# A transformer block on one core: out-projection by seven block products, and two norms left to the scales of later stages

## The chip, the cores and the metric

The kernel runs on one core of one Trainium2 chip. The metric is the device time of one execution in microseconds (us). TensorE multiplies (PE in the profile, with its weight loads as PEld), VectorE (DVE) and ScalarE (ACT) do elementwise work, GpSimd (POOL) does a little elementwise work and issues accumulating DMAs, and SyncE (SP) issues the other DMAs.

## The reference, cut to what matters

512 tokens of width 2048, 256 memory tokens, all float32. Three sub-layers, each with a norm before and a norm after it:

```python
h = rms_norm(x, g_mix_pre);  proj = h @ w_in            # 16 heads of 128
mix = concatenate([out_a, out_b], -1) @ w_out            # out-projection
x = x + rms_norm(mix, g_mix_post)
h = rms_norm(x, g_mem_pre)                               # cross-attention: 4 heads of 512
s_ = einsum(h @ w_mq, rms_norm(mem, g_mem_kv) @ w_mkv[keys]) * 512 ** -0.5
o = (softmax(s_) @ values) @ w_mo
x = x + rms_norm(o, g_mem_post)
h = rms_norm(x, g_ffn_pre)
gu = h @ w_gate_up
f = (silu(gu[:, :D_FF]) * gu[:, D_FF:]) @ w_down         # D_FF = 5632
x = x + rms_norm(f, g_ffn_post)
```

`rms_norm(x, g)` is x times 1/sqrt(mean(x*x) + eps) of its row, times g by column.

## The kernel before

Every fp32 operand is held as a high and a low part in fp32r, and a product is three matmuls in sequence: high by high, high by low, low by high. The making of such a pair is called a split: a copy on ScalarE and a subtraction on VectorE. Weights come in chunks of 128x1024 (512 KB). The class `Weights` loads them in a fixed order into five buffers (`NR`; eight from the end of cross-attention on) and splits each two chunks ahead of its use; `mm` (L218) issues the matmuls.

The stages are, in order: keys and values of the memory tokens, 16 attention heads, out-projection (about 880 to 1024 us in the profile), cross-attention (to about 1410) and the feed-forward part (FFN).

- **Out-projection.** `tok_ticks` runs over 4 blocks of 512 output columns by 8 weight chunks by 4 tiles of 128 tokens. The last column block is done twice over, for tiles 0 and 1 and then for tiles 2 and 3, and its eight chunks are loaded twice. `split_mix` splits the heads' outputs. `Sub.evict` squares the result for the norm behind it and multiplies by the gain `g_mix_post`.
- **The chain of a token tile** (`Sub.chain`): `residual` makes the row's 1/rms (`r1`, a power on POOL), adds x and squares the sum; `normed` makes the second 1/rms (`r2`) and, by column block, `h = y * r2 * gain` (L843, VectorE), the next sub-layer's normed input; `turn` transposes it on TensorE (L852) and splits it.
- **Cross-attention.** `fold_keys` multiplies `w_mq` by the keys (16 folds of 24 matmuls 128x256 for a pair of heads; in pair 0 the chains run between them), then come the scores, the softmax, `fold_values` (values by `w_mo`) and `cross_out`, which does all four tiles of a column block at once, and in the last column block one tile after the other, with a chain behind each.
- **FFN.** `Blocks` multiplies a 2x2 block matrix by seven products instead of eight (Strassen's method, Winograd's form): sums of blocks of the activations and of the weights first, sums of the products behind them. A block is 256 tokens by 1024 inputs by 512 columns; a product is 48 matmuls of 128x512. Weight sums are formed by accumulating DMAs, which POOL issues, or by VectorE.

Each engine works its instructions off in a fixed order. The order is set when the program is built: the code is written with generators (`side`, `side2`) that are advanced one step at each `fill()` between matmuls, and a scheduler merges what results.

Of the kernel before, what the change touches and what calls it, by code (L numbers as in the profile page):

```python
# [53 lines left out]
HOMES = {1: (0, 0), 2: (1, 0), 5: (0, 1), 6: (1, 1)}  # L54
# [4 lines left out]
SY, SZ = 5, 2  # L59
# [6 lines left out]
G_MIX, G_KV, G_DIFF, G_SB, G_ALL = 0, 16, 32, 33, 34  # L66

GP_MIX, GP_MEM, GP_FFN, GP_MEM_PRE, GP_FFN_PRE = range(5)


class Weights:
# [5 lines left out]
    def __init__(self, nc, raw, parts, chunks):  # L77
        self.nc, self.parts, self.chunks = nc, parts, chunks
        self.free = deque(raw[:, i] for i in range(NR))
# [10 lines left out]
    def more(self, tiles, mark):  # L90

        for t in tiles:
            self.nc.vector.tensor_copy(t[:, 0:1], mark[:, 0:1])
            self.free.append(t)

    def load(self, last):
        while self.loaded <= min(last, len(self.chunks) - 1):
            n = self.loaded
            _, how, *src = self.chunks[n]
            if how == "load":  # L100
                if not self.free:
                    return
                t = self.free.popleft()
                self.nc.sync.dma_start(t, src[0])
                for x in src[1:]:
                    self.nc.gpsimd.dma_start(t, x, accum_op=ALU.add)
                self.raw[n] = t
            self.loaded += 1

    def split(self, n):  # L110
        if n < len(self.chunks):
            r = self.raw.pop(n)
# [5 lines left out]
            if n in self.sums:  # L118
                m = self.sums[n]
                t = self.raw[m] = self.held.pop(self.chunks[m][2])  # L120
                self.nc.vector.tensor_tensor(t, t, r, op=ALU.add)
            if n in self.adds:
                m = self.adds[n]
                self.nc.gpsimd.dma_start(r, self.chunks[m][3], accum_op=ALU.add)  # L124
                self.raw[m] = r
            elif n in self.kept:
                self.held[n] = r
            else:
                self.free.append(r)
# [14 lines left out]
class Side:  # L144

    def __init__(self):
        self.q = deque()
        self.wait = 0  # L150
# [4 lines left out]
    def force(self):  # L155
        try:
            self.wait = next(self.q[0]) or 0
# [3 lines left out]
    def step(self):  # L161
        if self.wait:
            self.wait -= 1
        elif self.q:
# [5 lines left out]
    def drain(self):  # L170
        while self.q:
            self.force()
        self.wait = 0
# [3 lines left out]
def encoder_kernel(ctx: ExitStack, tc: tile.TileContext, a: dict, out: bass.AP):  # L177
# [69 lines left out]
    def wf(name, cbs, c0, n, order, make, again=False):  # L247
# [6 lines left out]
        for i in order:  # L254
            how, *x = make[i]
            for c in range(n):
                key = (name, cbs, c0 + c)
                if how == "load":
                    x_ = (block(c, *x[0]),)
# [15 lines left out]
    dn_cbs = [(0, 1), (2, 3)]  # L275
# [8 lines left out]
    for cb in range(NCB):  # L284
        wm("w_out", cb, range(8))
    wm("w_out", NCB - 1, range(8))
# [8 lines left out]
    for b, n in enumerate(DOWN):  # L295
        for cbs in dn_cbs:
            if (b, cbs) == (len(DOWN) - 1, dn_cbs[-1]):
# [11 lines left out]
    def fill():  # L309
        if later:  # L310
            later.popleft()()
        side.step()
        side2.step()
# [213 lines left out]
    mixT, mixhl = {}, {}  # L527
# [77 lines left out]
    def subnorm(o, head, g):  # L605
# [7 lines left out]
        yield 2  # L613
# [10 lines left out]
        m = u(s="mixT")  # L624
        nc.vector.scalar_tensor_tensor(m, ob, g, t, op0=ALU.mult, op1=ALU.mult)
        mixT[head] = m
        if head == 0:
            mixhl[0] = (u(F32R, "mixh"), u(F32R, "mixl"))
            split(*mixhl[0], mixT.pop(0))
# [72 lines left out]
    def sb_gen(h, q, k, v):  # L702
# [30 lines left out]
        yield SY  # L733
# [35 lines left out]
    def split_mix(kt):  # L769
        m = mixT.pop(kt)  # L770
        split(big[:, 0, kt], big[:, 1, kt], m)
        mixhl[kt] = from_big(kt)

# [3 lines left out]
    class Sub:  # L777
# [3 lines left out]
        def __init__(self, gp, src, dst, gpre, raw=None):  # L781
            self.gp, self.src, self.dst, self.gpre = gp, src, dst, gpre
            self.raw = raw
# [8 lines left out]
        def load_g(self, cb):  # L792
# [4 lines left out]
            if self.gpre is not None and cb == NCB - 1:  # L797
                self.gpre_rows = []
                for c in range(NCB):
                    t = u(s="gpre")  # L800
                    dma(t, a["grows"][self.gpre, c * 512 : (c + 1) * 512].partition_broadcast(P))
                    self.gpre_rows.append(t)
# [14 lines left out]
        def residual(self, t, steps=False):  # L817
# [5 lines left out]
            for cb in range(NCB):  # L823
                if cb == 2 and steps:
                    yield
                y, x = self.y[t, cb], self.x.pop((t, cb))
                if self.gpre is None and t >= NT - 2 and cb == 0:
# [4 lines left out]
                if self.gpre is not None:  # L832
# [3 lines left out]

        def normed(self, t, ss2):
            s2, r2 = st(), st()
            nc.vector.tensor_reduce(s2, ss2, axis=AX.X, op=ALU.add)
            pow_rstd(r2, s2, 1)  # L840
            for cb in range(NCB):
                h = u(s="h")
# [657 lines left out]
```

## Time and profile before

| What | Value |
|---|---|
| median of 3 runs | 2742.3 us (2740.06 to 2749.47) |
| the profiled execution | 2740.57 us, of which the span of the profile is 2738.8 |
| TensorE busy | 2674.0 us, 98% of the span |
| VectorE, ScalarE, GpSimd busy | 60%, 47%, 8% |
| mean granted TensorE clock | 0.991 of full speed |

The 1.8 us between the execution and the span lie around the profiled part. Waits of TensorE and stretches at a lower clock are what the span holds beside matmuls at full speed; the rows further down show them by stage.

### The profile page before, as it was taken

The numbers are of one execution on the slowest core, as the hardware profiler recorded it, in microseconds if no ns is written. First come the engines' busy times: TensorE is split into PE (matmuls) and PEld (weight loads), VectorE is DVE, ScalarE is ACT, GpSimd is POOL, SyncE is SP. The second block draws the span as 40 slices with busy tenths as digits, with TensorE's granted clock in tenths as the row PEclk, the third lists the DMA queues.
The fourth block names the chain that finished last, engine by engine and source line by source line (L and its number), as shares of the span: only waits on it lengthen the run. The fifth ranks groups of instructions, "written<-read, shape, count | busy, mean of one in ns | idle before, by whom it ended". The sixth has DMA issues, their size and how long they took to land.

```text
span 2738.8 us, 33641 instructions
## 1 busy us (share of the span) xinstructions
PE 2674.0 (98%) x12704; PEld 2220.3 (81%) x12704; DVE 1642.1 (60%) x2267; ACT 1296.7 (47%) x1908; POOL 230.7 (8%) x273
## 2 busy tenths in 40 slices
PE   8999999999999998999989999999999999999996
PEld 7888877888887788988877888888888888878775
DVE  6763555554444357335377655555555568787887
ACT  6542444445455345324365444444444456454553
POOL 0000000000000000000011122111121121101101
PEclk9999999999999999999999999999999999999998
DMA  8873222222222375223368999888888998778776
GB/s 304 293 255 98 84 89 85 81 82 76 81 73 74 115 249 193 67 100 124 113 202 188 252 207 209 205 205 204 206 195 208 200 229 247 208 251 206 197 206 204
DMA packets 163715, 470.14 MB, mean 172 GB/s; under 512 B 18272, under 2 KB 28920, under 8 KB 163552
## 3 DMA queue, kind: packets, MB, share of 16 engines
q1 hardware_dynamic: 128928, 346.45, 37.4%
q0 software_dynamic: 34624, 121.54, 24.1%
q8 instruction: 99, 1.62, 0.2%
q14 instruction: 64, 0.52, 0.1%
HBM read 431.20 MB, written 39.34 MB: 172 GB/s over the span
## 4 chain that ended last, share of the span: by engine, by line
PE 89%; issue 4%; DVE 3%; DMA 2%; ACT 1%; POOL 1%; SPq 0%; POOLq 0%; DVEq 0%; ACTq 0%
PE ps L218 88%; DVE parts L116 1%; PE ps L1251 1%; DMA aq<-actT_d 1%; PE ps L852 1%; ACT parts L115 1%; DMA xnat<-in_x_dram 1%; DMA raw<-in_w_dn_dram 0%; DVE y L831 0%; PE ps L689 0%; POOL y_d L1367 0%; DMA xres<-x_d 0%; DMA raws<-in_w_mk_dram 0%; DVE big L222 0%; DVE form L222 0%
## 5 line engine op out<-in xcount | busy, mean ns | idle before, releaser
L218 PE MATMUL ps<-parts,big 128*128 128x512 f32 x4992 | 1170.7, 392 | 12.9 <-ACT parts L115 7.0
L218 PEld LDWEIGHTS ps<-parts,big 128*128 128x128 f32 x4992 | 935.2, 188 | 214.6 <-DVE parts L116 9.5
L116 DVE TENSOR_TENSOR parts<-raws,parts 128x1024 fp32r<-128x1024 f32 x551 | 672.8, 1223 | 612.4 <-ACT parts L115 604.3
L115 ACT CAST parts<-raws 128x1024 fp32r<-128x1024 f32 x551 | 579.7, 1052 | 768.2 <-PE ps L218 698.8
L218 PE MATMUL ps<-parts,form 128*128 128x512 f32 x2376 | 551.3, 390 | 2.5 <-ACT parts L115 2.3
L218 PEld LDWEIGHTS ps<-parts,form 128*128 128x128 f32 x2376 | 444.5, 188 | 96.9 <-ACT parts L115 4.5
L218 PE MATMUL ps<-big,parts 128*128 128x512 f32 x1536 | 375.1, 394 | 0.0
L218 PEld LDWEIGHTS ps<-big,parts 128*128 128x128 f32 x1536 | 282.6, 188 | 61.9 <-issue 4.2
L116 DVE TENSOR_TENSOR parts<-raw,parts 128x1024 fp32r<-128x1024 f32 x175 | 213.8, 1223 | 150.7 <-ACT parts L115 150.5
L115 ACT CAST parts<-raw 128x1024 fp32r<-128x1024 f32 x175 | 184.3, 1054 | 203.5 <-PE ps L218 161.6
L218 PE MATMUL ps<-memhl,parts 128*128 128x512 f32 (+1 forms) x1024 | 182.1, 339 | 7.9 <-DVE memhl L229 7.3
L218 PEld LDWEIGHTS ps<-memhl,parts 128*128 128x128 f32 x1024 | 157.6, 190 | 31.7 <-DVE memhl L229 7.6
L124 POOL DMA_DIRECT2D raws<-in_w_gu_dram x112 | 96.8, 864 | 897.5 <-DVE parts L116 683.3
L369 POOL TENSOR_TENSOR small<-small 128x1 f32<-128x1 f32 (+2 forms) x22 | 16.8, 770 | 991.8 <-DVE small L368 976.4
L218 PE MATMUL ps<-khl,parts 128*128 128x256 f32 x768 | 96.9, 287 | 0.0
L218 PEld LDWEIGHTS ps<-khl,parts 128*128 128x128 f32 x768 | 94.6, 194 | 0.2
L218 PE MATMUL ps<-gh,big 128*128 128x512 f32 x256 | 80.0, 393 | 0.0
L218 PE MATMUL ps<-big,pTh 128*128 128x512 f32 x256 | 79.6, 390 | 0.0
L124 POOL DMA_DIRECT2D raw<-in_w_gu_dram x60 | 51.8, 864 | 111.5 <-DVE parts L116 111.5
L666 ACT ACTIVATE e<-e,small 128x512 f32<-128x512 f32 (+3 forms) x64 | 35.4, 555 | 54.2 <-DVE small L664 54.2
L814 DVE TENSOR_TENSOR y<-ps,gpost 128x512 f32<-128x512 f32 x32 | 22.0, 690 | 58.2 <-ACT junk L812 57.6
L218 PEld LDWEIGHTS ps<-gh,big 128*128 128x128 f32 x256 | 48.6, 190 | 10.1
(781 smaller groups left out, 2138.1 us busy)
## 6 DMA issues: line engine op xcount, KB each, us to landing
raws<-in_w_gu_dram POOLq DMA_DIRECT2D x113, 512.0 KB, 5.6
raws<-in_w_gu_dram SPq DMA_DIRECT2D x79, 512.0 KB, 4.3
raws<-in_w_qk_dram SPq DMA_DIRECT2D x64, 512.0 KB, 3.3
raw<-in_w_gu_dram POOLq DMA_DIRECT2D x63, 512.0 KB, 5.6
raw<-in_w_gu_dram SPq DMA_DIRECT2D x57, 512.0 KB, 4.1
aq<-actT_d SPq DMA_DIRECT2D x82, 256.0 KB, 5.8
raws<-in_w_dn_dram SPq DMA_DIRECT2D x41, 512.0 KB, 5.1
raws<-in_w_out_dram SPq DMA_DIRECT2D x40, 512.0 KB, 3.6
```

Source lines behind the costliest of these rows:

```text
L115: self.nc.scalar.copy(h, r)
L116: self.nc.vector.tensor_tensor(l, r, h.bitcast(F32), op=ALU.subtract)
L124: self.nc.gpsimd.dma_start(r, self.chunks[m][3], accum_op=ALU.add)
L218: nc.tensor.matmul(o, l, r, start=start, stop=stop, skip_group_check=True)
L369: nc.gpsimd.tensor_tensor(dst, t, mhalf[:, 0:n], op=ALU.pow)
L666: nc.scalar.activation(es[m][:, 0:n], es[m][:, 0:n], AF.Exp, bias=nmx[:, m : m + 1], accum_out=z[:, m : m + 1],)
L814: nc.vector.tensor_tensor(y, p, self.g[cb], op=ALU.mult)
L852: nc.tensor.transpose(tp[:, k * P : (k + 1) * P], h[:, k * P : (k + 1) * P], ident)
L1251: nc.tensor.transpose(tp[:, k * P : (k + 1) * P], f[:, k * P : (k + 1) * P], ident)
```

## The change

Three things change:

1. **The out-projection goes through `Blocks`.** Its columns are two pairs of blocks, `(0, 1)` and `(2, 3)`; each pair takes seven products of 48 matmuls. Products 1 and 7 of both pairs come first (`EARLY`), then 2, 3, 5, 6 and 4 of pair 0 and then of pair 1. The heads' outputs stay in 16 tiles `mix` of 128x2x256; `mix_forms` makes the activation blocks' sums, the subtractions on POOL (`sub_p`). Weights of products 7 and 5 are formed by a load and an accumulating DMA, of product 6 by VectorE, of product 4 by an accumulating DMA on what 6 used. Three more buffers (`mraw`) join once product 7 of pair 1 is out, until the out-projection ends. Behind the products, sums with product 7 (`last`) and the gain for tiles 2 and 3 run on POOL.
2. **No normed input is formed.** The rows `h` (L843) and the loads of their gains are gone. `turn` transposes the residual sum itself. The gain `g_mem_pre` is folded into the scale with which `fold_keys` splits its result, and `r2` becomes the scale of the softmax's exponent; `g_ffn_pre` is applied when the transposed tile leaves PSUM (a VectorE multiplication in the place of a ScalarE copy), and `r2` in the Silu's scale and in the gated product. A chain handles one tile and yields for stated times (`CH`) instead of numbers of steps.
3. **Cross output by tiles.** Column blocks 0 and 1 are done for all tiles as before, then blocks 2 and 3 for tile 0, then for tile 1, then block 2 and then block 3 for tiles 2 and 3. The subtractions of `late_forms` (FFN forms of tiles 2 and 3) move from VectorE to POOL.

```diff
-HOMES = {1: (0, 0), 2: (1, 0), 5: (0, 1), 6: (1, 1)}
+HOMES = {1: (0, 1), 2: (1, 1), 5: (0, 0), 6: (1, 0)}
+EARLY, ORDER_MIX = (1, 7), (2, 3, 5, 6, 4)
+MAKE_MIX = {1: ("load", (0, 0)), 7: ("load", (1, 1), (0, 1)), 2: ("load", (1, 0)),
+            3: ("load", (1, 1)), 5: ("load", (0, 0), (0, 1)), 6: ("sum", 3, 5),
+            4: ("add", 6, (1, 0))}
+CH = 8.0, 2.0
...
-        m = u(s="mixT")
-        nc.vector.scalar_tensor_tensor(m, ob, g, t, op0=ALU.mult, op1=ALU.mult)
+        for th in range(2):
+            if head % 2 == 0:
+                mix[head // 2, th] = u2(F32, "mix")
+            r = slice(th * M, (th + 1) * M)
+            nc.vector.scalar_tensor_tensor(
+                mix[head // 2, th][:, head % 2], ob[:, r], g, t[:, r],
+                op0=ALU.mult, op1=ALU.mult,
+            )
...
-        def normed(self, t, ss2):
...
-                nc.scalar.copy(self.raw[cb, t], tp)
+                nc.vector.tensor_tensor(
+                    h.rearrange("p (a b) -> p a b", a=4),
+                    tp.rearrange("p (a b) -> p a b", a=4),
+                    gain.unsqueeze(2).to_broadcast([P, 4, P]),
+                    op=ALU.mult,
+                )
...
+        def chain(self, t):
+            ss2 = yield from self.residual(t, True)
+            yield CH[0]
+            for cb in range(NCB):
+                self.turn(t, cb)
+                if cb == NCB - 1:
+                    s2, r2 = st(), st()
+                    nc.vector.tensor_reduce(s2, ss2, axis=AX.X, op=ALU.add)
+                    pow_rstd(r2, s2, 1)
+                    self.r2[t] = r2
+                yield CH[1]
...
+                    def last():
+                        nc.gpsimd.tensor_tensor(v, v, w, op=ALU.add)
+                        nc.gpsimd.tensor_tensor(r, r, w, op=ALU.add)
...
+    def mix_forms():
+        for k2 in range(1, 4):
+            mix_form(1, k2, mix[k2, 0])
+            yield 2
+        for k2 in range(4):
+            t = u2(F32, "s7")
+            sub_p(t, mix[k2, 1], mix[k2, 0])
+            mix_form(7, k2, t)
+            yield 2
+        for k2 in range(4):
...
+            a11, a12, a21, a22 = (mix.pop((k2 + 4 * c, r)) for r in range(2) for c in range(2))
+            mix_form(2, k2, a12)
+            sub_p(a21, a21, a22)
...
+            sub_p(a11, a11, a21)
...
+            sub_p(a12, a12, a11)
...
+            (nc.vector if t < 2 else nc.gpsimd).tensor_tensor(c, c, sub.g[cb], op=ALU.mult)
+            sub.y[t, cb] = c
+            if cb == col_pairs[-1][t < 2]:
+                (side, side2)[t // 2].add(sub.chain(t))
...
+    for i in EARLY:
+        for n, g in enumerate(pairs):
+            g.product(i)
+            done_mix.add((i, n))
+    mix_raw = [wpool.tile([P, 1024], F32, tag=f"mraw{i}", name=f"mraw{i}") for i in range(NR, NW)]
+    W.more(mix_raw, pairs[1].T[7, 1], n_mix)
...
-        split_scaled(gh, gl, p, 512 ** -0.5)
+        split_scaled(gh, gl, p, gmem[:, r : r + 1])
...
-            sub2(s, a21, a22)
+            sub_p(s, a21, a22)
...
+    for toks, cbs in (((0,), last), ((1,), last), ((2, 3), last[:1]), ((2, 3), last[1:])):
...
-            nc.scalar.activation(g, g, AF.Silu)
-            nc.vector.tensor_tensor(f, f, g, op=ALU.mult)
+            nc.scalar.activation(g, g, AF.Silu, scale=sub3.r2[t])
+            nc.vector.scalar_tensor_tensor(f, f, sub3.r2[t], g, op0=ALU.mult, op1=ALU.mult)
```

In the built programs TensorE has 12634 matmuls where it had 12730, and the 96 that are gone are matmuls of 128x512 in the out-projection. Its weight chunks go from 40 to 56: SP issues 40 loads for them as before, and POOL 24 accumulating DMAs of 512 KB, eight of them for product 7, eight for 5, eight for 4. POOL has 48 more elementwise operations of 128x512 (16 subtractions for the forms of the out-projection, 16 in `late_forms`, 8 additions in `last`, 8 gain multiplications). VectorE loses the 32 rows `h` and has 16 more weight splits, 8 weight sums of 128x1024 and 16 multiplications at the transposes' eviction ahead of the FFN.

How the order moves, at three places. First TensorE in the folds of `w_mq` (`ps<-khl,parts`), up to the first transposes of a tile there in the row that begins with L852 (L854 in the changed kernel). Before:

```order
L218 MATMUL ps_7959<-khl_7391,parts 128x256 x3
L218 MATMUL ps_7959<-khl_7452,parts 128x256 x3
L218 MATMUL ps_7959<-khl_7453,parts 128x256 x3
L852 MATMUL ps_7988<-small,h_7916 128x128 x4
L218 MATMUL ps_7998<-khl_7266,parts 128x256 x3
L218 MATMUL ps_7998<-khl_7267,parts 128x256 x3
```

And in the changed kernel, at the first transposes of tile 2:

```order
L233 MATMUL ps_8053<-khl_7733,parts 128x256 x3
L233 MATMUL ps_8053<-khl_7734,parts 128x256 x3
L233 MATMUL ps_8053<-khl_7771,parts 128x256 x3
L233 MATMUL ps_8053<-khl_7772,parts 128x256 x3
L854 MATMUL ps_8097<-small,p__807_6674 128x128 x4
L233 MATMUL ps_8107<-khl_7649,parts 128x256 x3
```

The transposes read the residual sum (here `p__807_6674`, a product's tile) and no `h`. This row of tile 2 stands behind product 4 of pair 1 (48 matmuls), four folds and four groups of transposes, and ahead of the first transposes of tile 1.

Second POOL from the attention heads to the FFN; L369 and L388 are powers on small columns, L474 is a preparation of the lambdas, L124 and L136 issue accumulating DMAs for the FFN's weights. Before:

```order
L369 TENSOR_TENSOR small<-small 128x4
L474 TENSOR_TENSOR small<-small 128x2
L369 TENSOR_TENSOR small<-small 128x1 x8
L124 DMA raws<-in_w_gu_dram 128x1024 x3
L369 TENSOR_TENSOR small<-small 128x1 x8
L124 DMA raws<-in_w_gu_dram 128x1024 x6
```

In the changed kernel, from the last accumulating DMA for `w_out` on, around the end of the out-projection:

```order
L136 DMA mraw_7027<-in_w_out_dram 128x1024
L1007 TENSOR_TENSOR p__831_6816<-p__831_6816,p__854_7023 128x512
L1007 TENSOR_TENSOR p__832_6818<-p__832_6818,p__855_7025 128x512
L1006 TENSOR_TENSOR p__911_7701<-p__911_7701,p__854_7023 128x512
L1006 TENSOR_TENSOR p__912_7703<-p__912_7703,p__855_7025 128x512
L388 TENSOR_TENSOR small<-small 128x1
L1079 TENSOR_TENSOR p__911_7701<-p__911_7701,gpost_7456 128x512
L1079 TENSOR_TENSOR p__912_7703<-p__912_7703,gpost_7456 128x512
L388 TENSOR_TENSOR small<-small 128x1 x2
L1079 TENSOR_TENSOR p__831_6816<-p__831_6816,gpost_7453 128x512
L1079 TENSOR_TENSOR p__832_6818<-p__832_6818,gpost_7453 128x512
```

Where POOL had only the powers of the chains, four additions and four multiplications of 128x512 now stand among them, and the powers of the later tiles stand behind those.

Third TensorE where the FFN begins (`ps<-parts,big` are its products, `ps<-big,pTl` the last matmuls of `cross_out`, `h` and `y` what is transposed). Before:

```order
L218 MATMUL ps_10699<-big,pTl_9719 128x512
L852 MATMUL ps_10734<-small,h_10644 128x128 x4
L852 MATMUL ps_10747<-small,h_10646 128x128 x4
L852 MATMUL ps_10788<-small,h_10780 128x128 x4
L852 MATMUL ps_10795<-small,h_10782 128x128 x4
L852 MATMUL ps_10802<-small,h_10784 128x128 x4
L852 MATMUL ps_10809<-small,h_10786 128x128 x4
L218 MATMUL ps_10826<-parts,big 128x512 x13
```

And in the changed kernel:

```order
L233 MATMUL ps_10891<-parts,big 128x512
L233 MATMUL ps_10892<-parts,big 128x512
L854 MATMUL ps_10986<-small,y_9964 128x128 x4
L854 MATMUL ps_10993<-small,y_9967 128x128 x4
L233 MATMUL ps_11004<-parts,big 128x512
L233 MATMUL ps_11005<-parts,big 128x512
L854 MATMUL ps_11018<-small,y_10222 128x128 x4
```

Before, six groups of transposes stand between the last matmul of `cross_out` and the first product. Now the transposes of tiles 2 and 3 stand behind some 40 matmuls of the first FFN product.

## Rows read from the trace of the kernel before

**Rows 1.** Busy time by stage; behind it TensorE's granted clock, DMA share, GB/s.

```profile
core 0: us, PE busy (x) PEld busy (x) DVE busy (x) ACT busy (x) POOL busy (x), PEclk, DMA share, GB/s
880.00:902.00 22.00, 17.74 (x66) 13.41 (x67) 8.83 (x12) 8.33 (x14) 0.00 (x0) 0.92 0.12 35
902.00:1000.00 98.00, 97.94 (x432) 80.73 (x432) 36.15 (x40) 31.40 (x50) 0.00 (x0) 1.00 0.49 166
1000.00:1024.00 24.00, 23.14 (x110) 18.99 (x109) 20.56 (x31) 13.91 (x24) 2.22 (x3) 1.00 0.86 309
1024.00:1087.00 63.00, 55.44 (x436) 54.87 (x435) 52.39 (x79) 41.27 (x74) 4.23 (x5) 0.94 0.62 209
1395.00:1455.00 60.00, 48.07 (x229) 38.98 (x228) 53.94 (x91) 45.46 (x84) 4.08 (x7) 0.91 0.58 182
1600.00:2000.00 400.00, 400.00 (x1807) 332.07 (x1806) 229.81 (x236) 189.00 (x217) 72.12 (x84) 1.00 0.88 204
```

**Rows 2.** What TensorE waited for, 880 to 1455 us.

```profile
engine line waited for: us in total, times, longest us
PE ps L852 <- DVE h L843: 16.5, 3, 8.9
PE ps L218 <- ACT parts L115: 4.2, 3, 1.8
PE ps L218 <- ACT sqh L221: 2.0, 1, 2.0
PE ps L218 <- ACT big L221: 1.7, 2, 1.4
```

**Rows 3.** Busy time in the stretches of that time at half clock.

```profile
884.40:887.80 3.40, 3.40 (x9) 2.68 (x9) 0.00 (x0) 0.00 (x0) 0.00 (x0) 0.50 0.00 0
1041.40:1044.80 3.40, 3.40 (x19) 3.40 (x18) 3.00 (x7) 0.42 (x1) 0.32 (x1) 0.50 0.56 227
1082.40:1089.20 6.80, 5.33 (x21) 4.97 (x22) 6.46 (x12) 3.06 (x6) 0.00 (x0) 0.50 0.71 231
1406.70:1416.90 10.20, 4.93 (x20) 4.67 (x21) 9.07 (x24) 9.88 (x27) 2.10 (x4) 0.50 0.94 317
```

**Rows 4.** TensorE in order of time in the folds.

```profile
start us, us, engine line op out<-in xcount [idle before <-releaser]
1045.77 3.12 PE L218 MATMUL ps<-khl,parts 128*128 128x256 f32 x24
1048.73 0.60 PE L852 MATMUL ps<-small,h 128*128 128x128 f32 x4
1049.08 3.11 PE L218 MATMUL ps<-khl,parts 128*128 128x256 f32 x24
```

**Rows 5.** VectorE in order of time, last 40 us.

```profile
2704.41 1.22 DVE L116 TENSOR_TENSOR parts<-raws,parts 128x1024 fp32r<-128x1024 f32 x1
2705.55 0.68 DVE L1202 TENSOR_TENSOR p__1821_19444<-p__1821_19444,base 128x512 f32<-128x512 f32 x1
2706.15 0.68 DVE L1202 TENSOR_TENSOR p__1822_19446<-p__1822_19446,base 128x512 f32<-128x512 f32 x1
...
2714.07 0.74 DVE L831 SCALAR_TENSOR_TENSOR p__1761_18881<-p__1761_18881,small,xres 128x512 f32<-128x512 f32 x1
...
2725.88 1.10 DVE L831 SCALAR_TENSOR_TENSOR p__1769_18949<-p__1769_18949,small,xres 128x512 f32<-128x512 f32 x1 [2.03 <-DMA xres<-x_d]
```

**Rows 6.** GpSimd in order of time, last 40 us.

```profile
2710.64 0.56 POOL L369 TENSOR_TENSOR small<-small 128x1 f32<-128x1 f32 x1 [15.23 <-DVE small L368]
2711.89 2.67 POOL L369 TENSOR_TENSOR small<-small 128x1 f32<-128x1 f32 x1 [0.69 <-DVE small L368]
...
2725.18 1.26 POOL L829 TENSOR_TENSOR r__1787_19084<-r__1787_19084,xres 128x512 f32<-128x512 f32 x1 [0.32 <-ACT r__1787_19084 L828]
```

**Rows 7.** DMA queues: packets, MB, share of 16 engines' time.

```profile
q1 hardware_dynamic: 128928, 346.45, 37.4%
q0 software_dynamic: 34624, 121.54, 24.1%
```

**Rows 8.** DMA issues: count, size, median us from issue to landing.

```profile
raws<-in_w_gu_dram POOLq DMA_DIRECT2D x113, 512.0 KB, 5.6
raws<-in_w_out_dram SPq DMA_DIRECT2D x40, 512.0 KB, 3.6
raws<-in_w_dn_dram POOLq DMA_DIRECT2D x30, 512.0 KB, 8.6
```

More of the change, by code (lines that the diff above doesn't have):

```diff
@@ L78, in __init__ @@
         self.nc, self.parts, self.chunks = nc, parts, chunks
-        self.free = deque(raw[:, i] for i in range(NR))
+        self.free = deque((raw[:, i], len(chunks)) for i in range(NR))
         self.raw, self.held, self.ready = {}, {}, {}
@@ L88, in __init__, with more @@
                 self.sums[x[1]] = n
-    def more(self, tiles, mark):
+    def more(self, tiles, mark, until=None):
         for t in tiles:
             self.nc.vector.tensor_copy(t[:, 0:1], mark[:, 0:1])
-            self.free.append(t)
+            self.free.append((t, len(self.chunks) if until is None else until))
     def load(self, last):
@@ L149, in __init__ @@
         self.q = deque()
-        self.wait = 0
+        self.wait, self.time = 0, 0.0
     def add(self, gen):
@@ L172, in drain @@
             self.force()
-        self.wait = 0
+        self.wait, self.time = 0, 0.0
 @with_exitstack
@@ L796, in load_g @@
             self.g[cb] = t
[L797 to L802, printed above, removed]
         def load_x(self, t):
@@ L864, in turn, with need @@
             )
-        def chain(self, toks):
-            for t in toks:
-                ss2 = yield from self.residual(t, True)
-                yield 1
-                self.normed(t, ss2)
-                yield 3
-                for cb in range(NCB):
-                    self.turn(t, cb)
-                    yield 1
-    sub = Sub(GP_MIX, a["x"], x2_d, GP_MEM_PRE)
+        def chain(self, t):
[9 more added lines that the diff above has]
+                yield CH[1]
+        def need(self, t):
+            while t not in self.r2:
+                for s in (side, side2):
+                    if s.q:
+                        s.force()
+    sub = Sub(GP_MIX, a["x"], x2_d)
     khl = {}
@@ L921, in encoder_kernel @@
-        side.add(sub.chain(toks))
+            g.product(i)
+    while later:
+        later.popleft()()
     sub.load_x(3)
-    mixhl.clear()
     G = {}
+    gmem = st(KT)
+    nc.vector.tensor_scalar(gmem, gains[:, G_MEM : G_MEM + KT], 512 ** -0.5, None, op0=ALU.mult)
     def fold_keys(pair, r):
@@ L1070, in home, with ffn_part @@
         return homes[n]
+    def ffn_part(i, kt, t):
+        return (x[:, kt % 4] for x in forms[i, kt // 4, t])
     def form(i, g, t, src, nk=4, pin=lambda ins: ins):
@@ new lines, in encoder_kernel @@
+        if cbs[-1] == last[1]:
+            if toks[0] == 2:
+                more = [
+                    wpool.tile([P, 1024], F32, tag=f"raw{i}", name=f"raw{i}")
+                    for i in range(NR, NW)
+                ]
+                W.more(more, sub.y[3, last[1]])
+            for t in toks:
+                s = (side, side2)[t % 2]
+                if t == 3:
+                    sub.load_x(t)
+                s.add(sub.chain(t))
+                s.add(early_forms(t) if t < 2 else late_forms(t - 2))
@@ L1345, in encoder_kernel @@
         for i in ORDER[:2]:
+            for t, s in enumerate((side, side2)):
+                while (i, 1, t) not in forms:
+                    s.force()
             g.product(i)
     side.drain()
+    side2.drain()
     for j, cbs in enumerate(gu_cbs):
@@ L1391, in encoder_kernel @@
         last = b == len(DOWN) - 1
-        for cbs in dn_cbs:
-            end = last and cbs == dn_cbs[-1]
+        for cbs in col_pairs:
+            end = last and cbs == col_pairs[-1]
             if last:
```

458 lines of the change are left out of this document (246 added, 212 removed).

## The prediction

> **What bounds the kernel now.** I read the stages first [rows 1], then what TensorE waits for in them [rows 2], then its clock [rows 3]. In most of the feed-forward part TensorE is the whole time: 400.00 us busy of 400. The same holds for the middle of the out-projection, 97.94 of 98. So a matmul that is left out there is worth its place in the row, and not the 390 ns or so that one takes with its overlaps: 97.94 / 432 = 0.227 us. A wait that is left out is worth its length. The waits sit at the changed code: idle TensorE time is 22.00 − 17.74 = 4.26 us at the entry of the out-projection, 0.06 and 0.86 in it, 7.56 in the folds behind it, and 11.93 around the entry of the FFN. Of these, 16.5 us in three waits are transposes that wait for the normed rows `h` [rows 2]; 2.0 at the first entry wait for the last head's squares (`sqh`), 4.2 for weight splits, and 1.4 of the 1.7 on `big` stand alone in `load_values`, between scores and `fold_values`. Together 24.7 + 1.4 = 26.1 us.
>
> Behind each long wait the granted clock reads 0.50, the level of 1.2 GHz against 2.4, for some 3 to 10 us [rows 3]. TensorE was idle just before it fell, and busy before it rose. While it is busy in them, half the time is lost: (3.40 + 3.40 + 5.33 + 4.93) / 2 = 8.5 us. By place, waits plus clock are: head entry 4.26 + 1.70 = 6.0; out-projection and folds 0.06 + 0.86 + 7.56 + 1.70 + 2.67 = 12.8; `load_values` 1.4; FFN entry 11.93 + 2.47 = 14.4. The sum is 34.6 us, and it is all that this change can find besides matmuls.
>
> **Part 1, fewer matmuls.** The order shows 96 matmuls of 128x512 fewer. 96 × 0.227 = 21.8 us. This part is nearly certain, since the FFN runs the same seven products without idle time [rows 1].
>
> **Part 1, what supplies them.** A product is 48 matmuls, 48 × 0.227 = 10.9 us, and eats four chunks, one each 2.72 us. At first there are five buffers, so a buffer comes round after 13.6 us. In the products 7 it must hold a load of 3.6 us, an accumulation of 5.6 (rows of like kind) [rows 8] and a split of about 1.22 on ScalarE and then VectorE each [rows 5], 11.6 in all. That fits, with 2 us to spare. In bytes: SP's 40 loads are 21 MB, and at the hardware queue's 0.374 × 2738.8 / 346.45 = 2.96 us per MB [rows 7] take 62 us of all engines; POOL's 24 accumulations are 12.6 MB, and at 0.241 × 2738.8 / 121.54 = 5.43 us per MB take 68. That is 130 us of the 14 × 10.9 = 153 us which the products last, a share of 0.85. The out-projection has 0.49 now; the FFN has 0.88 and loses nothing [rows 1]. So I count the supply as hidden, and its failing as a rival.
>
> At the head entry, in the new order the matmul on `sqh` has some 30 product matmuls (6.8 us) ahead of it. Its own 2.0 us should go; what stays lies between 0 and today's 6.0. I take 4, since the other pieces of that chain still end in a wait.
>
> **Part 1, VectorE in the products.** The price of back to back passes [rows 5] is the spacing of their starts: 128x1024 takes 2705.55 − 2704.41 = 1.14 us, 128x512 takes 0.60; one with a scalar counts as 0.74. From product 2 to product 4 of pair 0 VectorE has 26 of the first, 23 of the second and 3 of the third: 29.6 + 13.8 + 2.2 = 45.7 us, against five products of 54.4. If POOL's 11 operations in that stretch, 1.26 us each [rows 6], hold VectorE up for their whole time, 13.9 more make 59.6. The wait there is between 0 and 5.2; I take 3, because POOL's subtractions are early in that stretch and the forms of products 5, 6 and 4 hang on them.
>
> **The fold entry.** This is the place I am least sure of. Count from the start of the last product (4 of pair 1), where product 6's results come free. By the order VectorE has until tile 2's first residual row 9 passes of 128x1024, 15 of 128x512 and 8 with a scalar: 10.3 + 9.0 + 5.9 = 25.2 us, and that row itself 0.74: 25.9. A fold takes 1048.73 − 1045.77 = 2.96 and a group of four transposes 1049.08 − 1048.73 = 0.35 [rows 4], so TensorE reaches tile 2's transposes after 10.9 + 4 × 2.96 + 4 × 0.35 = 24.1. That leaves 1.8 us of wait at least. In the same stretch POOL has four additions and four multiplications of tiles 2 and 3, 8 × 1.26 = 10.1; if all of it is on the path, 11.9. I take 7 in the middle, and 2 for the clock behind it (4.4 today): 9 against 12.8. Tile 2 stands ahead of tile 1 on TensorE, so everything later waits with it. That `h` is not made is worth little here: 4 passes per tile leave VectorE, but splits of weight chunks take their place.
>
> That tiles 2 and 3 have their additions on POOL is the choice that can go wrong. The trace shows the two engines in each other's way at its end: a VectorE row that takes 0.74 alone (2714.07) took 1.10 when it began 0.7 us into a POOL operation of 1.26 (2725.88 against 2725.18) [rows 5, 6], and a POOL power of 0.56 took 2.67 behind back to back VectorE passes [rows 6].
> The Trainium skill, "SBUF — State Buffer", section "Who interferes with whom", says that a VectorE instruction with two SBUF inputs and a GpSimd instruction that reads SBUF exclude each other, and that whichever comes first holds the other up for its whole length. By this rule all 48 new POOL operations take from VectorE what they run, and rival c gets the more weight; the two rows above agree with it.
>
> **Scores, values, FFN entry.** The softmax scale adds one small VectorE operation per tile, `gmem` one in all; TensorE goes on with the next tile's scores meanwhile, so I count them at nothing; without that cover each costs less than the 0.60 of a 128x512 pass. `load_values` keeps its 1.4. At the FFN entry the transposes of tiles 2 and 3 today stand between the last cross matmul and the first product, and wait up to 8.9 us for `h` [rows 2]. In the new order they stand about 40 matmuls (9 us) into the first product, and wait for the residual alone. VectorE is 53.94 of 60 us busy there now [rows 1]; over the four tiles it loses 16 rows `h` of 0.74 and 16 subtractions of 0.60, and takes on 16 gain multiplications of 0.68. The 16 subtractions on POOL take 16 × 1.26 = 20.2. Between 0 and today's 14.4 I take 4: the cover of 9 us is about as long as the longest wait, but the forms of the first products still pass through VectorE.
>
> **The sum.** Waits and clock after: 4 + 3 + 9 + 1.4 + 4 = 21.4, that is 13.2 less than 34.6. With the matmuls, 21.8 + 13.2 = 35.0. 2740.57 − 35.0 = 2705.6; the median of the runs before is 1.7 above the profiled execution, so 2707.
>
> **The rivals.**
> (a) The forecast, 2699 to 2718 by the bounds of its terms taken a few at a time. Chance 0.53.
> (b) The waits really go. With the residual transposed directly and tiles finished one at a time, nothing of the 33.2 us at the three places stays: 2740.57 − 21.8 − 33.2 + 1.7 = 2687. For it: the largest wait of the kernel is on `h`, which no longer exists. Against it: the pass count at the folds. 0.22.
> (c) VectorE and POOL in turns become the bound: 48 × 1.26 = 60.5 us that VectorE can't use for two-input passes. Head entry 6.0 as today, pair 0 5.2, folds 11.9 + 4.4, values 1.4; at the FFN entry 20.2 on POOL in the place of 16 × 0.60 on VectorE adds 10.6 to 4 or to today's 14.4. Sum 43.5 to 53.9: 2740.57 − 21.8 − 34.6 + 43.5 + 1.7 = 2729 to 2740. It ends on the other side if the new waits pass 34.6 + 21.8 = 56.4, and if all 60.5 came on top of today's waits, at 2781. For it: the two rows of the end [rows 5, 6]. Against it: POOL's operations stand in stretches where VectorE's counts leave some room, and much of VectorE's work there reads PSUM or has one input from a weight buffer that waits for ScalarE anyway. 0.17, of which 0.05 faster, 0.08 same, 0.04 slower.
> (d) The supply is late: with an accumulation of 8.6 us, as at the down weights [rows 8], the round of a buffer in products 7 takes 14.6 instead of 13.6, about 1 us for each of eight chunks: 2707 + 8 = 2715. 0.08.
> That the change does not do what it says is excluded, since the order has 96 matmuls fewer.
>
> **Range and chances.** The likeliest case has 2707. Half of (b) below 2690 and the part of (c) above 2735 make up about 0.2, so the range is 2690 to 2735. A difference of 0.3% (8 us) is about what a measurement of this kernel can tell from none: faster means under 2734. (a), (b), (d) and 0.05 of (c) give 0.88; same 0.08; slower 0.04.
>
> **What would show it.** Right: TensorE has 12634 matmuls; no wait of a transpose on `h`; a wait of some 7 us at tile 2's transposes on a residual row (VectorE); half clock behind that alone; TensorE full in the two pairs' products; at the FFN entry single waits under 4 us. Wrong: weight splits of products 7 that wait for a DMA (d); VectorE rows of 128x512 with over 1 us each beside POOL's, and TensorE waiting for forms in pair 0 or in products 5, 7 and 6 of the FFN (c); none of these and no wait at the folds (b). If the sum of waits is as told but the time is not, the price of a matmul in a product is not 0.227.

## The result, and the profile after

The changed kernel takes 2754.6 us (median of 7 runs, 2750.3 to 2758.6) against 2741.3 for the kernel before: a ratio of 1.0046, 95% interval 1.0032 to 1.0060. It is slower by half a per cent, where 2707 was forecast.

The busy time by stage of the changed kernel, with the columns of [rows 1]; the stages are the head entry with products 1 and 7, the other products, the folds of pair 0, and the FFN entry:

```profile
827.80:930.00 102.20, 83.61 (x352) 67.08 (x351) 70.69 (x71) 58.69 (x89) 32.75 (x28) 0.88 0.66 172
930.00:1044.20 114.20, 101.39 (x404) 79.88 (x405) 83.67 (x98) 50.52 (x76) 33.45 (x25) 0.93 0.67 175
1044.20:1107.60 63.40, 55.55 (x450) 55.37 (x449) 55.60 (x84) 46.61 (x89) 13.52 (x11) 0.92 0.68 230
1424.00:1475.00 51.00, 42.37 (x191) 33.34 (x189) 49.13 (x55) 33.40 (x58) 32.89 (x21) 0.97 0.52 176
```

The idle time is 18.6, 12.8, 7.9 and 8.6 us. In [rows 1] the out-projection stood at 97.94 of 98; now neither of its two stages is full. The sum row over the nine stretches at half clock from 831.8 to 1459.9 us shows TensorE busy 38.09 of 54.65 us, so 19.0 us are lost to the clock, where [rows 3] gave 8.5:

```profile
sum 54.65, PE 38.09 PEld 31.73 DVE 50.68 ACT 20.44 POOL 20.15; mean PE 4.23 PEld 3.53 DVE 5.63 ACT 2.27 POOL 2.24
```

What TensorE waits for from 827 to 1044 us, to be held against [rows 2]:

```profile
PE ps L233 <- DVE parts L128: 16.3, 9, 4.3
PE ps L233 <- DVE big L237: 5.7, 1, 5.7
PE ps L233 <- ACT sph L236: 3.6, 3, 1.8
PE ps L233 <- ACT parts L127: 3.1, 4, 1.5
```

The wait on `h` is gone, but splits of weights (`parts`) and of activation forms (`big`) now end late. The reason shows in VectorE's and GpSimd's rows in order of time. VectorE in the changed kernel:

```profile
863.78 6.91 DVE L237 TENSOR_TENSOR big<-s,big 128x512 fp32r<-128x512 f32 x1 [2.30 <-ACT big L236]
...
871.22 2.86 DVE L237 TENSOR_TENSOR big<-s,big 128x512 fp32r<-128x512 f32 x1
...
875.13 0.68 DVE L237 TENSOR_TENSOR big<-mix,big 128x512 fp32r<-128x512 f32 x1
...
879.22 5.41 DVE L128 TENSOR_TENSOR parts<-raws,parts 128x1024 fp32r<-128x1024 f32 x1 [0.59 <-ACT parts L127]
...
925.69 2.28 DVE L133 TENSOR_TENSOR raws<-raws,mraw 128x1024 f32<-128x1024 f32 x1 [3.12 <-DMA mraw<-in_w_out_dram]
```

GpSimd there:

```profile
861.50 2.82 POOL L909 TENSOR_TENSOR s<-mix,mix 128x512 f32<-128x512 f32 x2
863.96 2.82 POOL L909 TENSOR_TENSOR mix<-mix,mix 128x512 f32<-128x512 f32 x2
866.41 1.21 POOL L118 DMA_DIRECT2D raws<-in_w_out_dram  x1
867.03 3.11 POOL L909 TENSOR_TENSOR mix<-mix,mix 128x512 f32<-128x512 f32 x2
869.94 1.03 POOL L118 DMA_DIRECT2D raws<-in_w_out_dram  x1
870.55 2.97 POOL L909 TENSOR_TENSOR mix<-mix,mix 128x512 f32<-128x512 f32 x2
```

And TensorE, with the waits at its rows:

```profile
870.75 7.35 PE L233 MATMUL ps<-parts,big 128*128 128x512 f32 x20 [5.75 <-DVE big L237]
...
884.68 2.50 PE L233 MATMUL ps<-parts,big 128*128 128x512 f32 x5 [4.35 <-DVE parts L128]
...
933.24 28.64 PE L233 MATMUL ps<-parts,big 128*128 128x512 f32 x116 [3.97 <-DVE parts L128]
```

A VectorE row of 0.68 us took 6.91, from 863.78 to 870.69; below, such a stretching is called a hold. In that time GpSimd went on through four more subtractions (863.96 to 870.14, by its rows) and two issues of DMAs, the second at 869.94. TensorE then had been idle for 5.75. The same happened at 879.22, with 4.35. The wait of 3.97 at 933 has another cause: the weight sum for product 6 (L133) stood in VectorE's queue and waited 3.12 for an accumulating DMA; the split that TensorE wanted stood behind it. The accumulating DMAs landed later than [rows 8] has it for the FFN (a median of 5.6 us): in the out-projection of the changed kernel the rows say

```profile
raws<-in_w_out_dram POOLq DMA_DIRECT2D x18, 512.0 KB, 7.0
mraw<-in_w_out_dram POOLq DMA_DIRECT2D x6, 512.0 KB, 8.5
```

### The profile page after: what moved, and what is told of

The parts are those of the page before. It is cut to its first block, busy times and chain, and to the rows that moved or that the text cites. A ratio compares the mean times of both kernels' runs of the same rounds, so it can differ in the third digit from the quotient of the medians.

```text
span 2755.4 us, 33701 instructions
## 1 busy us (share of the span) xinstructions
PE 2663.9 (97%) x12608; PEld 2205.2 (80%) x12608; DVE 1717.0 (62%) x2329; ACT 1322.9 (48%) x1936; POOL 336.0 (12%) x345
## 4 chain that ended last, share of the span: by engine, by line
PE 82%; DMA 5%; issue 5%; DVE 5%; ACT 1%; POOL 1%; SPq 0%; POOLq 0%; ACTq 0%; DVEq 0%
PE ps L233 80%; DVE parts L128 2%; DMA raws<-in_w_dn_dram 1%; DMA xres<-x_d 1%; DMA mraw<-in_w_out_dram 1%; ACT parts L127 1%; PE ps L1368 1%; DMA kraw<-kT_d 1%; DVE big L237 1%; DMA actT_d<-fT 0%; POOL y_d L1488 0%; DMA raw<-in_w_dn_dram 0%; DMA xnat<-in_x_dram 0%; PE ps L854 0%; DVE form L237 0%
## 5 line engine op out<-in xcount | busy, mean ns | idle before, releaser
L233 PE MATMUL ps<-parts,big 128*128 128x512 f32 x4824 | 1141.0, 394 | 38.2 <-DVE parts L128 24.1
L233 PEld LDWEIGHTS ps<-parts,big 128*128 128x128 f32 x4824 | 907.2, 189 | 239.6 <-DVE parts L128 33.9
L128 DVE TENSOR_TENSOR parts<-raws,parts 128x1024 fp32r<-128x1024 f32 x555 | 686.9, 1240 | 572.7 <-ACT parts L127 567.6
L136 POOL DMA_DIRECT2D raws<-in_w_gu_dram x112 | 97.8, 873 | 823.2 <-DVE parts L128 622.8
L233 PE MATMUL ps<-memhl,parts 128*128 128x512 f32 (+1 forms) x1024 | 184.0, 341 | 10.4 <-DVE memhl L244 8.8
L118 POOL DMA_DIRECT2D raws<-in_w_out_dram x12 | 11.0, 920 | 686.0 <-DMA raws<-in_w_out_dram 680.1
L136 POOL DMA_DIRECT2D raw<-in_w_gu_dram x60 | 52.4, 873 | 111.6 <-DVE parts L128 108.4
L136 POOL DMA_DIRECT2D raws<-in_w_dn_dram x30 | 26.2, 875 | 256.5 <-DVE parts L128 203.8
```

The source lines that it names most:

```text
L118: self.nc.gpsimd.dma_start(t[0], x, accum_op=ALU.add)
L128: self.nc.vector.tensor_tensor(l, r, h.bitcast(F32), op=ALU.subtract)
L233: nc.tensor.matmul(o, l, r, start=start, stop=stop, skip_group_check=True)
```

## The experiments

Theories: **X**, VectorE is held up by GpSimd's elementwise operations; **S**, the weights that accumulating DMAs form come late; **O** and **T**, the order that the merging of the generators makes is bad at single places. The kernel before ran beside each batch, at medians of 2741.1 to 2741.6. Behind each time stand, in brackets, its ratio to the kernel before and the 95% interval of that ratio. Names such as `all_dve` are those of the experiments; `sub2` and `add` run on VectorE, `sub_p` on GpSimd. Every edit changes the program that the scheduler merges, so the order can move at other places as well.

**GpSimd's operations on VectorE, in parts and all.** The subtractions of `mix_forms` alone (`mixsubs_dve`):

```diff
-            sub_p(t, mix[k2, 1], mix[k2, 0])
+            sub2(t, mix[k2, 1], mix[k2, 0])
...
-            sub_p(a21, a21, a22)
+            sub2(a21, a21, a22)
```

> The 16 subtractions for the out-projection's forms (sub_p in mix_forms) run on VectorE, all else as changed. Theory X (VectorE is held up while GpSimd runs its 128x512 operations): the VectorE rows of 6.91, 2.86 and 5.41 us near 864 to 885 us go back to about 0.7 to 1.2, the waits of 5.75 and 4.35 us on them and most of the half clock behind them go, and the time falls by 12 to 20 us, to 2735 to 2743. Theory S (the weights come late, and the rows are only where that shows): VectorE gets 16 more passes of 0.60, the waits on weight splits stay, and the time is 2752 to 2762. Theory O (the merged order itself puts waiting rows ahead): within 5 us of 2755.

2741.3 us (0.9998, 0.9989 to 1.0006), 13.3 under the changed kernel. Between 820 and 945 us no VectorE row takes more than 1.3 us there, so theory X holds at the place with the longest rows. The additions of product 7 and the gain of tiles 2 and 3 (`sums_dve`):

```diff
-                        nc.gpsimd.tensor_tensor(v, v, w, op=ALU.add)
+                        add(v, v, w)
...
-            (nc.vector if t < 2 else nc.gpsimd).tensor_tensor(c, c, sub.g[cb], op=ALU.mult)
+            nc.vector.tensor_tensor(c, c, sub.g[cb], op=ALU.mult)
```

> The 8 additions of product 7 (last) and the 8 gain multiplications of tiles 2 and 3 run on VectorE, the subtractions stay on GpSimd. Theory X: these 16 operations stretched VectorE rows by about 1.1 us each around 964 to 975, 1032 to 1038 and 1052 to 1058; the time falls by 3 to 8 us, to 2747 to 2752, above all at the wait of 7.9 us in the folds. Theory S: no change at 2755. A third: VectorE is full there, and 16 more passes of 0.60 cost it 5 to 10 us: 2760 to 2765.

2751.9 (1.0036, 1.0024 to 1.0048): 2.7 less, which is within the scatter of the single runs (2747.1 to 2757.0 against 2750.3 to 2758.6), and just short of the smallest gain that X was given. The fold's wait did not go with them; it grew from 7.9 to 9.0 us. Where this edit changes nothing, at 863 us, the row that took 6.91 in the changed kernel took longer still:

```profile
862.74 10.25 DVE L237 TENSOR_TENSOR big<-s,big 128x512 fp32r<-128x512 f32 x1 [2.87 <-ACT big L236]
```

So the length of such a hold is not fixed, even where the order of the instructions is the same. Both edits, and `late_forms` with `sub2` as well (`all_dve`):

> All 48 GpSimd operations of the change on VectorE (16 subtractions, 8 additions, 8 multiplications of the out-projection, 16 subtractions of late_forms). Theory X: 43 us of stretched VectorE rows become 48 x 0.60 = 29 us of passes without stalls that others wait for; the time falls by 20 to 35 us, to 2720 to 2735, faster than before. Theory S: 2750 to 2765.

2729.3 (0.9957, 0.9945 to 0.9969), 25.3 less than the changed kernel and faster than before. No VectorE row is stretched in the out-projection, the folds or the FFN entry any more. So the same work is cheaper on the fuller engine.

**The accumulating DMAs.** The weight sums of products 7, 5 and 4 are not formed here (`no_accum`):

```diff
-MAKE_MIX = {1: ("load", (0, 0)), 7: ("load", (1, 1), (0, 1)), 2: ("load", (1, 0)),
-            3: ("load", (1, 1)), 5: ("load", (0, 0), (0, 1)), 6: ("sum", 3, 5),
-            4: ("add", 6, (1, 0))}
+MAKE_MIX = {1: ("load", (0, 0)), 7: ("load", (0, 1)), 2: ("load", (1, 0)),
+            3: ("load", (1, 1)), 5: ("load", (0, 1)), 6: ("sum", 3, 5),
+            4: ("load", (1, 0))}
```

> The 24 accumulating DMAs of the out-projection are left out: products 7, 5 and 4 take one plain load per chunk, so the weight sums are not formed; the sums for product 6 stay, and SP issues 48 loads. Theory S: the waits on weight splits near 880, 926 to 933 and 988 to 992 and the clock behind them go, 20 to 30 us: 2725 to 2735. Theory X: only the waits behind sums that wait for a DMA go (929, 989, 992: some 7 us with clock), and the rest stays: 2745 to 2751.

2730.9 (0.9956, 0.9944 to 0.9968): 23.7 less, what S forecast. But GpSimd's subtractions were all still there, and VectorE's rows grew by at most 1.1 us each; these are the longest near the place of the long holds:

```profile
861.89 2.32 DVE L128 TENSOR_TENSOR parts<-raws,parts 128x1024 fp32r<-128x1024 f32 x1
864.13 1.78 DVE L237 TENSOR_TENSOR big<-mix,big 128x512 fp32r<-128x512 f32 x1
```

So the DMA issues also have to do with the long holds. Both edits together (`all_dve_no_accum`):

> All 48 operations on VectorE, and the 24 accumulating DMAs left out as well (the weight sums of products 7, 5 and 4 are not formed). If the two causes (VectorE held up by GpSimd; accumulated weights late) are separate, the gains of 25 and 24 us add: 2706, which is what was predicted for the change. If they are one chain (late weights keep GpSimd's queue back and bunch its subtractions, or both stand in the same stalls), only a part adds: 2715 to 2725.

2714.9 (0.9902, 0.9887 to 0.9917). The gains of 25.3 and 23.7 make 39.8 together, so some 9 us are shared. Read the other way: without the accumulating DMAs the 48 operations still cost 16.0 us on GpSimd (2730.9 against 2714.9), though no row grows by more than 1.1 us; with all 48 on VectorE the DMAs still cost 14.4 (2729.3 against 2714.9). So 16 of GpSimd's 25 us need no long hold; rows that are each held by a little are enough.

**The order of the sums.** As `all_dve`, and (`all_dve_sums_pinned`):

```diff
-                self.nc.vector.tensor_tensor(t, t, r, op=ALU.add)
+                ins = self.nc.vector.tensor_tensor(t, t, r, op=ALU.add)
+                if self.chunks[n][0][0] == "w_out":
+                    self.pin(ins)
```

where `pin` keeps an instruction behind the one ahead of it in the code. The VectorE rows of `all_dve` show what it is about:

```profile
906.70 0.69 DVE L912 TENSOR_TENSOR mix<-mix,mix 128x512 f32<-128x512 f32 x1
910.50 1.23 DVE L133 TENSOR_TENSOR raws<-raws,mraw 128x1024 f32<-128x1024 f32 x1 [3.11 <-DMA mraw<-in_w_out_dram]
911.64 1.22 DVE L128 TENSOR_TENSOR parts<-mraw,parts 128x1024 fp32r<-128x1024 f32 x1
```

> All 48 operations on VectorE, and the weight sums for product 6 kept behind the instruction that stands ahead of them in the code (the split of product 5's chunk), in place of the merged order that puts them ahead of splits. Theory H (sums that wait for an accumulating DMA hold up the splits behind them on VectorE): the waits of 3.6, 1.6 and 1.5 us near 913, 973 and 981 us and the half clock behind the first go, and the time falls by 6 to 10 us to 2719 to 2723. Theory S (the chunk itself is late): the wait moves to the split, 2726 to 2732.

2722.8 (0.9932, 0.9920 to 0.9945), 6.5 less: theory H. The waits of 3.6, 1.6 and 1.5 us are gone; the longest at those places is 1.05. A sum whose chunk is split only some 20 us later (the accumulation behind that split is issued at 932.3 us in `all_dve`) had held up a split that was needed at once.

**Parts 2 and 3 of the change alone.** The out-projection of before (`tok_ticks`, `split_mix`), all else as changed (`norms_cross_only`):

> The out-projection of before with parts 2 and 3 of the change (no normed rows, chains by tile, cross output by tiles, late_forms on GpSimd). My forecast's terms give the folds 12.8 to 9, the FFN entry 14.4 to 4: 2727. From the trace of the changed kernel, with its FFN 5 us shorter, cross output 2.5 us longer and folds as long: 2738.

2727.7 (0.9948, 0.9936 to 0.9961): 13.3 less than before, at the time that the forecast's terms gave, but by luck: the folds have no idle time at all where 9 us of waits and clock were forecast, and the FFN entry is idle for 7.45 us and stands at a clock of 0.91 where the forecast had 4 for both. And with the subtractions of `late_forms` on VectorE (`norms_cross_late_dve`):

> As norms_cross_only, and the 16 subtractions of late_forms on VectorE. Theory X: 15 us of stretched VectorE rows go at the FFN entry, and with them waits of some 9 us: 2728 to 2731, 7 to 10 us less than norms_cross_only. If VectorE is full there: the same time or more.

2722.0 (0.9926, 0.9914 to 0.9939): 5.7 less again, just outside what X was given. In its windows, too, the folds have no idle time, and the FFN entry 4.1 us:

```profile
1025.00:1080.00 55.00, 55.00 (x450) 54.34 (x449) 45.70 (x66) 41.59 (x73) 4.20 (x5) 1.00 0.66 228
1393.00:1448.00 55.00, 50.93 (x234) 40.09 (x233) 52.53 (x82) 38.65 (x63) 3.93 (x6) 1.00 0.59 192
```

In `norms_cross_only` the second row reads

```profile
1393.00:1448.00 55.00, 47.55 (x203) 37.60 (x202) 53.01 (x61) 35.26 (x61) 32.89 (x21) 0.91 0.53 173
```

and GpSimd issues no DMA among its 16 subtractions there. VectorE's rows beside them grew by at most 1.1 us each, as these two do, so the 5.7 us are the price of short holds alone:

```profile
1425.03 1.75 DVE L237 TENSOR_TENSOR big<-s,big 128x512 fp32r<-128x512 f32 x1
1432.94 2.31 DVE L128 TENSOR_TENSOR parts<-raw,parts 128x1024 fp32r<-128x1024 f32 x1
```

**Tile 2's place in the folds.** The wait at tile 2's first transposes is there with all operations on VectorE too, as TensorE's rows in `all_dve_sums_pinned` show:

```profile
1035.69 1.09 PE L857 MATMUL ps<-small,p__807_6674 128*128 128x128 f32 x4 [8.37 <-DVE p__807_6674 L847]
```

As `all_dve_sums_pinned`, with (`pinned_tile2_later`)

```diff
-                (side, side2)[t // 2].add(sub.chain(t))
+                (side, side2)[t // 2].add(sub.chain(t, 9.0 if t == 2 else 0.0))
```

where the number is a first pause of the chain, in us of TensorE's work:

> As all_dve_sums_pinned, and the chain of tile 2 begins 9 us of TensorE's time later, so that its first transposes stand 8 to 9 folds into the folds instead of 4 to 5, behind tile 1's first. Theory T (the wait of 8.4 us at tile 2's transposes and the half clock behind it come from their place on TensorE): some 8 us of wait and 3 of clock go: 2710 to 2714. Theory V (VectorE is full at the folds, and the wait only moves): 2719 to 2724.

2712.5 (0.9892, 0.9878 to 0.9905), 10.3 less: theory T. This version leaves out nothing of the computation and beats both kernels. The folds now read 50.46 us busy of 52:

```profile
1018.00:1070.00 52.00, 50.46 (x420) 49.55 (x420) 50.60 (x84) 44.54 (x87) 5.91 (x7) 1.00 0.78 267
```

The delay alone, in the changed kernel (`tile2_later_only`):

> The changed kernel with that delay of tile 2's chain alone, all 48 operations still on GpSimd. Theory T: 2741 to 2747, some 10 us under the changed kernel. If GpSimd's eight operations there are what makes tile 2 late: 2750 to 2756, since they hold VectorE up wherever the transposes stand.

2748.8 (1.0024, 1.0014 to 1.0035): 5.8 less, between what the two were given. The wait of 7.9 is gone there, but one of 2.4 us on a weight split stands in the folds. In the profiled execution, the slowest of its eight, the entry of the out-projection had a wait of 9.1 where the changed kernel had 5.75: the delay does not touch that place, but the row of 6.91 took 10.25 here, as it did in `sums_dve`.

**GpSimd against VectorE by itself.** The kernel before, with two bursts of 16 subtractions on finished tiles, whose results are not read (`before_gpsimd_bursts`):

```diff
+            if cb in (1, 2) and c == 2:
+                for i in range(16):
+                    d = u(s="d")
+                    nc.gpsimd.tensor_tensor(
+                        d, sub.y[i % 4, cb - 1], sub.y[i % 4, cb - 1], op=ALU.subtract
+                    )
```

> The kernel before, with two bursts of 16 GpSimd subtractions of 128x512 on finished tiles, whose results nothing reads, in the middle of the out-projection where TensorE was busy 97.94 of 98 us. Theory X: each burst takes some 20 us, a VectorE row with two SBUF inputs in it takes up to that long, and TensorE runs out of split chunks: 10 to 15 us a burst with the clock, 2760 to 2772. If GpSimd does not hold VectorE up: 2741.

2743.4 (1.0007, 0.9997 to 1.0016): a miss. VectorE's rows grew by at most 0.9 us each. So the long holds of the changed kernel are more than two engines taking turns. Two variants (`before_bursts_two_inputs` and `before_bursts_with_dmas`):

> As before_gpsimd_bursts, but each of the 32 subtractions reads two different tiles. There VectorE got in after one GpSimd operation, and its rows grew by some 0.6 us. If two inputs make GpSimd keep VectorE out for several operations: VectorE rows of 5 us and more in the bursts, and 2748 to 2765. If not: rows longer by 0.6 to 1.3 us, 2740 to 2745.

> As before_bursts_two_inputs, with a plain GpSimd DMA of 256 KB ahead of each two subtractions, kept in that order. In the changed kernel the VectorE rows of 2.86 to 6.91 us stood where GpSimd's subtractions alternate with DMA issues, and without those issues no row grew by more than 1.2 us. If DMA issues among the operations make the long holds: VectorE rows of 3 to 10 us in the bursts, and 2745 to 2765. If not: as without the DMAs.

2744.3 (1.0010, 1.0000 to 1.0019) and 2742.7 (1.0003, 0.9994 to 1.0013); the second expectation came true for the rows and missed for the time. VectorE's rows in the first burst with two inputs:

```profile
912.12 1.78 DVE L116 TENSOR_TENSOR parts<-raws,parts 128x1024 fp32r<-128x1024 f32 x1 [6.36 <-ACT parts L115]
917.56 2.32 DVE L116 TENSOR_TENSOR parts<-raws,parts 128x1024 fp32r<-128x1024 f32 x1 [3.66 <-ACT parts L115]
```

With DMA issues among the subtractions:

```profile
911.30 3.61 DVE L116 TENSOR_TENSOR parts<-raws,parts 128x1024 fp32r<-128x1024 f32 x1 [4.83 <-ACT parts L115]
916.75 1.75 DVE L116 TENSOR_TENSOR parts<-raws,parts 128x1024 fp32r<-128x1024 f32 x1 [1.83 <-ACT parts L115]
922.18 8.53 DVE L116 TENSOR_TENSOR parts<-raws,parts 128x1024 fp32r<-128x1024 f32 x2 [3.69 <-ACT parts L115]
```

A row of 1.22 takes 3.61, and the last two take 8.53 together. The long hold is there, so DMA issues among the subtractions make it. Yet the time does not move: from 820 to 1025 us TensorE waits 2.0 us for VectorE's splits where it waits 0.9 in the kernel before, so the out-projection of before hides it.

**What the supply costs in the best version.** Without the accumulations of product 7 (`pinned_tile2_no_accum7`), then without all 24 (`pinned_tile2_no_accum`), again with those weight sums not formed:

> As pinned_tile2_later, with the eight accumulating DMAs of product 7 left out (its weight sum is not formed), the 16 of products 5 and 4 kept. If the late supply of the first four products with five buffers is what is left of it: 5 to 8 us under pinned_tile2_later. If it is the products 5 and 4 of the pairs: within 2 us of it.

2711.1 (0.9890, 0.9876 to 0.9903): 1.4 less than `pinned_tile2_later`, which is within the scatter of the runs.

> pinned_tile2_later with all 24 accumulating DMAs left out (the weight sums of products 7, 5 and 4 are not formed). It measures what the supply still costs there: leaving out those of product 7 alone gave 1.4 us. If products 5 and 4 carry the rest of the supply's cost: 2703 to 2707. If not: 2709 to 2712.

2707.2 (0.9872, 0.9857 to 0.9886): 5.3 less than `pinned_tile2_later`, of which product 7 has at most a small part. The supply of products 5 and 4 carries the rest.

## Why the prediction was wrong, by its steps

**The price of a matmul fits.** 96 matmuls less were to be worth 21.8 us where nothing waits. `pinned_tile2_no_accum`, without the supply's cost, is 14.8 us under `norms_cross_late_dve`, and most of the missing 7.0 are small waits: from 820 to 1110 us TensorE is idle for 9.28 us in the one and 4.55 in the other (no wait over 1.7 us in the first), and its stretches at half clock lose 3.3 us against 1.7.

**Waits and clock after** were forecast at 21.4 and are 68. By place, idle time plus half of the busy time at half clock:

| Place | Forecast | Measured |
|---|---|---|
| entry, products 1 and 7 | 4 | 18.6 + 7.6 = 26.2 |
| products 2 to 4 of both pairs | 3 | 12.8 + 7.1 = 19.9 |
| folds | 9 | 7.85 + 2.7 = 10.5 |
| `load_values` | 1.4 | 1.4 |
| FFN entry | 4 | 8.6 + 1.7 = 10.3 |

Before's span less 21.8 and 34.6 and plus 68.3 is 2750.7; the span was 2755.4, so 4.7 us lie elsewhere. Idle time ahead of these stages is 2.4 of them (10.4 us up to 827 us against 8.0 before); the rest is not placed.

**The step that failed first is "the head entry".** It looked at the matmul on `sqh` alone. That wait did vanish, but the forms of products 1 and 7 and the first subtractions of product 2 came to stand there, 13 subtractions on GpSimd among eight accumulating DMAs, and no term was made for them. That was the place of the 13.3 us of `mixsubs_dve`, and the entry with products 1 and 7 took 26.2 where the forecast had 4.

**"I count the supply as hidden"** failed by 24 us in this kernel, by 14.4 with GpSimd's operations on VectorE, and by 5 in the best version. The accumulation was taken at 5.6 us from the FFN's row and took 7.0 and 8.5. The round of a buffer in products 7 was not the trouble: by its own terms it still fits with 7.0 (3.6 + 7.0 + 2.4 = 13.0 of 13.6 us), and leaving those accumulations out gave 1.4 us in the best version. What was not reckoned is who else stands in a queue behind a late chunk: the sum on VectorE (6.5 us, by pinning), and GpSimd's own subtractions, which come behind issues that wait for loads and then run one after another.

**The folds** came out near the size forecast, but not for the reason. GpSimd's eight operations are not it: with them on VectorE the wait was 9.0. The order that the prediction named itself, tile 2 ahead of tile 1, was worth 10.3 us once those operations were on VectorE, and 5.8 in the changed kernel. That `h` is not made was called worth little there. With the out-projection of before, parts 2 and 3 take the folds' whole wait away; how much of that is `h` and how much the chains by tile, no run separates.

**The FFN entry** was forecast at 4 and has 10.3. The 16 subtractions on GpSimd cost 5.7 us against VectorE, by `norms_cross_late_dve`, which with 4.1 us of idle time and a full clock is what the forecast had. Parts 2 and 3 together gave 13.3, as much as all of the forecast's savings in waits, in other places.

**The rivals.** (c) was the mechanism with most in it, at 2729 to 2740 and a chance of 0.17; a slower kernel had 0.04. Its price failed where it kept the head entry at today's 6.0, and in taking GpSimd's operations one by one, each stopping VectorE for its own length, which the long holds pass by far; and it was not joined with (d), which was given 8 us. The point at which it turns (56.4 us of waits) was passed by 12. The rule cited from the Trainium skill, "SBUF — State Buffer", section "Who interferes with whom", agrees with the bursts without DMAs, where a row grew by no more than one GpSimd operation; with DMA issues among them the rows grew by several, which is more than the rule says. One of the two rows that the prediction read as agreeing with that rule showed as much, with the engines the other way round: GpSimd's power of 0.56 us that took 2.67 from 2711.89 on [rows 6] outlasted three VectorE rows, not one:

```profile
2711.73 1.21 DVE L116 TENSOR_TENSOR parts<-raws,parts 128x1024 fp32r<-128x1024 f32 x1
2712.87 0.68 DVE L1077 TENSOR_TENSOR p__1809_19332<-p__1809_19332,base 128x512 f32<-128x512 f32 x1
2713.47 0.68 DVE L1371 TENSOR_TENSOR p__1821_19444<-p__1821_19444,gpost 128x512 f32<-128x512 f32 x1
```

**Why the same hold costs here and not in before** is argued, not shown. A chunk feeds 24 matmuls in the old out-projection (5.4 us) and 12 in a product (2.7), and is split two chunks ahead: the cover is about 11 us there and 5.4 here. The bursts' two rows of 8.53 us fit under the one; the split that took 5.41 at 879.22 fills the other, and a wait of 4.35 came of it.

## What to carry to other kernels

Halving the work per weight chunk also halves the time by which splits run ahead, if the argument above is right, so ask for each queue what its longest single hold may be, not only whether its total fits. An operation moved to a nearly idle GpSimd is dear when the fuller VectorE is next in the chain, and dearer when GpSimd also issues DMAs among such operations; here the moves cost some 25 us, 16 of them without those DMAs, and paid nothing. A row that waits for a DMA should stand in an in-order queue behind what is needed sooner: look in the trace for a short row with a DMA's wait ahead of rows that TensorE wants.

## What the runs showed of the hardware

GpSimd subtractions of 128x512 in sequence take turns with VectorE rows that have two inputs in SBUF: in the burst with two inputs such a row grew by 1.1 us at most, and a GpSimd one from 1.29 to 2.27. A VectorE row with an input in PSUM was not held: L752 (`e<-ps,e`) took its 0.68 us at 870.62 in the changed kernel, beside a subtraction. With GpSimd DMA issues between the subtractions (0.55 to 1.2 us each) VectorE got in only after several: 6.91 us for a row of 0.68 in the changed kernel and 10.25 for the same row in two others, 3.61 for one of 1.22 in the bursts. What inside GpSimd makes the difference, the runs don't show.
